# A fused SSM, attention and FFN layer: first steps in a stated order, narrow products for the SSM's outputs, and weights and parameters laid out on the host

## The chip, the cores and the metric

The kernel runs on one core of a Trainium2 chip. The metric is the device time of one execution in microseconds, as the median of several runs. The core has five engines that run their own instruction lists in order: PE (TensorE, products and transposes), DVE (VectorE), ACT (ScalarE), POOL (GpSimd) and SP (SyncE, here only an issuer of DMAs). They wait for one another by semaphores. DMAs are issued by SP, ACT and POOL.

## The reference, cut to what matters

All is float32. There are 256 prompt tokens and 8 samples of 4 tokens, 288 columns together; the model is 2048 wide, the FFN 5632, and the SSM has 64 groups of 16 channels with 64 complex states each.

```python
x = x + 0.5 * swiglu(rms_norm(x, ffn1_norm), ffn1_w_gate, ffn1_w_up, ffn1_w_down)
z = rms_norm(x, mix_norm) @ w_in                       # u, q, k, v, qi, ki, wi, ga, gb
lam_bar = exp(lam * dt); b_bar = ((lam_bar - 1) / lam)[..., None] * b
h = associative_scan(h[t] = lam_bar * h[t-1] + b_bar @ u[t])
y = real(c @ h) + d * u                                # the SSM's outputs
za = gelu(y); a = za * sigmoid(za @ glu_w + glu_b)
b = sparse_attention(q, k, v, top_k by indexer(qi, wi, ki))
x = x + (sigmoid(ga) * (a @ w_branch_a) + sigmoid(gb) * (b @ w_branch_b)) @ w_out
x = x + 0.5 * swiglu(rms_norm(x, ffn2_norm), ffn2_w_gate, ffn2_w_up, ffn2_w_down)
```

## The kernel before

Activations stay in SBUF with channels on the 128 partitions and the 288 tokens as columns. A weight matrix is streamed in chunks of 512 rows by 256 columns (512 KB): SP loads a chunk into a `raw` tile (`fetch`, L208, four buffers), ACT casts it to `whi` (L216) and DVE takes the remainder as `wlo` (L217; `parts`, three buffers each). The activations are split the same way into `hh` and `hl` (or `hi` and `lo`). `project` then makes three products per 128 rows of weights, high by high, high by low and low by high (L240, L241, L242), each 288 columns wide. Of these main products there are 17328 in all, 96 of them from `project_first` (L274 to L276).

PE's instructions run in the order in which the program was written. Those of the other engines are ordered by a scheduler with priorities; `high_priority(offset=FIRST)` lifts the casts and copies that main products need.

`project_first` computes the first 256 columns of the first gate matrix while x arrives. `load_x` loads x in 256-column pieces (`xa`, L304) and the sample rows in pieces of 32 by 128 (`xb`, L309). `turn(k)` transposes the k-th of 16 tiles of x on PE (L316, twice) and brings in the sample columns by products with the identity (L317). ACT scales the tile by the norm's gain into `hh` (L320), DVE forms `hl` (L321), and x itself is copied by ACT for even k and by DVE for odd k (L322). The weights come in steps of 2, 2, 4, 4 and 4 row blocks. The next projection, of w_up, follows directly; for the norm ACT squares the 16 tiles of x (`sq`, L383) and DVE adds them up (`ssq`, L384).

Everything else is side work: Python generators, of which `tick` advances each by one step after every second row block of a projection, so that their instructions fall between main products. `prepare` is such a generator. It loads constants and parameters on ACT's queue, turns norm vectors from rows to columns by transposes on PE (`rows` and `turned`, L347), computes the SSM's discretization, transposes five parameter tables (L653), shuffles b and loads c with short runs (L717, L722), and for each of eight channel blocks `c8` transposes a piece of C (L751) and builds the tables `in`, `chunk`, `out` and `turn`, which go to DRAM. The page table is loaded as `pti` by eight small DMAs (L595) and cast by DVE (L641).

`ssm` is the generator that uses the tables, a software pipeline (`pipe`) of 16 steps n, one each 20 ticks, two steps to a block c8. A stage is given by its lag in ticks. `out` (lag 37) multiplies by `chunk` and `out`: 8 float32 products with the 72 columns of inputs or states as weights and 64 moving columns (L930, L931), after which ACT copies the result, tokens on partitions, to Y. `back` (lag 42) turns a pair's Y with four transposes (L944), and ACT applies GELU. A float32 product is two entries on PE, which the trace's rows count.

Of the kernel before, what the change touches and what calls it, by code (L numbers as in the profile page):

```python
# [13 lines left out]
I32 = mybir.dt.int32  # L14
# [39 lines left out]
L_BIT = 3  # L54

# [63 lines left out]
class Net:  # L119
    def __init__(self, ctx, tc, D):  # L120
# [5 lines left out]
        self.wide, self.turn, self.under_way = True, False, False  # L126
        self.const = ctx.enter_context(tc.tile_pool(name="const", bufs=1))
# [93 lines left out]
    def project(self, w, c0, n, xs):  # L221
# [25 lines left out]
    def project_first(self, w, c0, xs):  # L247

        nc = self.nc
# [3 lines left out]
        raws = {}  # L253

        def fetch(i):
            k0, kt = steps[i]
            raws[i] = self.fetch(w[k0 * P:(k0 + kt) * P, c0:c0 + 256], kt, 256, nc.sync if i else nc.scalar)
        for c, i in enumerate((0, 1, 2, None, 3, None, None, None)):
            if i is not None:
                fetch(i)  # L260
            if c < 7:
                self.load(c + 1)
        xs[1]
        self.warm(2)
        for i, (k0, kt) in enumerate(steps):
            more = steps[i + 1][1] if i + 1 < len(steps) else 0
            if i == 0:
                fetch(4)
            hi, lo = self.parts(raws.pop(i))
            for j in range(2):  # L270
                for k in range(kt):
# [20 lines left out]
    def load_x(self, xp, xs, g):  # L292

        nc = self.nc
        w = 256
        ctx = ExitStack()
        pool = ctx.enter_context(self.tc.tile_pool(name="xin", bufs=1, side="right"))
        rows, some = {}, {}
        self.x = [None] * 16

        def load(c):
            rows[c] = [pool.tile([P, w], F32, name=self.name("xa")) for _ in range(2)]
            for i, a in enumerate(rows[c]):
                nc.sync.dma_start(a, xp[i * P:(i + 1) * P, c * w:(c + 1) * w])  # L304
            if c % 2 == 0:

                some[c // 2] = pool.tile([P, P], F32, name=self.name("xb"))
                for j in range(4):
# [1177 lines left out]
```

## Time and profile before

| | |
|---|---|
| median of 3 runs | 2496.82 us (2496.34 to 2498.28) |
| profiled run | 2496.11 us, its span 2494.3 us |
| PE busy | 2471.9 us, 99% of the span |
| DVE, ACT, POOL busy | 1529.0 (61%), 1083.6 (43%), 171.5 (7%) us |
| mean DMA rate | 177 GB/s |
| weight loads from issue to landing, median | 3.2 to 4.8 us |
| mean granted TensorE clock | 0.999 of full speed |

A PE row of the timeline gives a product's start and duration. Consecutive products overlap, so the time that a product adds is the distance from its start to the next start. Names such as `xa` or `wlo` are the program's tiles. "x4" after a row counts instructions of one kind in a row. What stands in brackets is idle time of the engine ahead of the row, and the last release that ended it.

### The profile page before, as it was taken

The page shows a single profiled execution, that of the slowest core. Times are in us where ns is not written, and L with a number is a line of the kernel's source. Part 1 is how long each engine was busy: PE and PEld are TensorE (multiplying, and loading weights), DVE is VectorE, ACT ScalarE, POOL GpSimd, SP SyncE. Part 2 cuts the span into 40 slices and gives each one's busy share as a digit, 9 for nine tenths or more (in the row PEclk, how much of TensorE's full clock was granted, in tenths as well). Part 3 has the DMA queues.
Part 4 walks back from the last instruction along what each step waited for, and adds up shares of the span by engine and source line. Part 5 has one row for each costly group of instructions (what it writes and reads, how often), then busy time and mean ns, then how long its engine had stood idle before and what let it go on. Part 6 is the DMA issues. An engine that isn't in the chain of part 4 may idle for free.

```text
span 2494.3 us, 46557 instructions
## 1 busy us (share of the span) xinstructions
PE 2471.9 (99%) x18859; PEld 2432.3 (98%) x18859; DVE 1529.0 (61%) x2889; ACT 1083.6 (43%) x1605; POOL 171.5 (7%) x270
## 2 busy tenths in 40 slices
PE   8999999999999999999999999999999999999999
PEld 8999999999999999999899999999999999999999
DVE  6658787875555656789555457556555454554555
ACT  5433334333333445455865634344333333333333
POOL 1001033221000001000023210000000000000000
PEclk9999999999999999999999999999999999999999
DMA  6456666666545655446477676555555555555554
GB/s 198 155 167 156 191 189 193 191 198 193 162 153 178 198 171 184 135 147 201 139 222 234 199 237 224 173 163 167 163 167 168 162 169 166 164 169 163 161 172 134
DMA packets 441962, 441.36 MB, mean 177 GB/s; under 512 B 35002, under 2 KB 432532, under 8 KB 441748
## 3 DMA queue, kind: packets, MB, share of 16 engines
q1 hardware_dynamic: 424608, 413.47, 52.7%
q0 software_dynamic: 11552, 21.32, 2.9%
q10 hardware_dynamic: 5588, 3.61, 0.5%
q8 instruction: 148, 2.42, 0.4%
q14 instruction: 66, 0.54, 0.1%
HBM read 418.48 MB, written 19.83 MB: 176 GB/s over the span
## 4 chain that ended last, share of the span: by engine, by line
PE 93%; DVE 2%; DMA 2%; ACT 1%; issue 1%; POOL 0%; SPq 0%; ACTq 0%; POOLq 0%; DVEq 0%
PE acc L240 16%; PE acc L242 16%; PE acc L241 16%; PE psy L240 13%; PE psy L242 13%; PE psy L241 13%; DVE wlo L217 1%; DMA kv<-in_cache_v,idx 1%; PE aux L1301 1%; DMA raw<-in_ffn_w_gate 0%; DMA cn<-in_ssm_c_re 0%; PE aux L1142 0%; ACT whi L216 0%; PE aux L1347 0%; PE aux L1311 0%
## 5 line engine op out<-in xcount | busy, mean ns | idle before, releaser
L217 DVE TENSOR_TENSOR wlo<-raw,whi 128x1024 fp32r<-128x1024 f32 (+1 forms) x741 | 885.9, 1196 | 752.8 <-ACT whi L216 736.5
L216 ACT CAST whi<-raw 128x1024 fp32r<-128x1024 f32 (+1 forms) x741 | 761.2, 1028 | 1165.3 <-PE acc L241 461.7
L240 PE MATMUL acc<-hh,whi 128*128 128x288 f32 x2240 | 679.1, 303 | 0.0
L242 PE MATMUL acc<-hh,wlo 128*128 128x288 f32 x2240 | 661.1, 295 | 4.6 <-DVE wlo L217 4.6
L241 PE MATMUL acc<-hl,whi 128*128 128x288 f32 x2240 | 661.4, 295 | 0.0
L240 PE MATMUL psy<-hh,whi 128*128 128x288 f32 (+1 forms) x1520 | 454.1, 299 | 0.3 <-DVE g L429 0.3
L241 PE MATMUL psy<-hl,whi 128*128 128x288 f32 (+1 forms) x1520 | 448.5, 295 | 0.0
L242 PE MATMUL psy<-hh,wlo 128*128 128x288 f32 (+1 forms) x1520 | 448.2, 295 | 0.0
L240 PEld LDWEIGHTS acc<-hh,whi 128*128 128x128 f32 x2240 | 421.7, 188 | 8.1 <-issue 7.4
L242 PEld LDWEIGHTS acc<-hh,wlo 128*128 128x128 f32 x2240 | 422.3, 189 | 5.3 <-DVE wlo L217 5.3
L241 PEld LDWEIGHTS acc<-hl,whi 128*128 128x128 f32 x2240 | 422.5, 189 | 1.2 <-issue 0.7
L240 PE MATMUL psy<-hi,whi 128*128 128x288 f32 x992 | 294.0, 296 | 0.0
L240 PE MATMUL acc<-hi,whi 128*128 128x288 f32 x992 | 293.8, 296 | 0.0
L241 PE MATMUL psy<-lo,whi 128*128 128x288 f32 x992 | 292.4, 295 | 0.0
L241 PE MATMUL acc<-lo,whi 128*128 128x288 f32 x992 | 292.4, 295 | 0.0
L242 PE MATMUL acc<-hi,wlo 128*128 128x288 f32 x992 | 292.1, 294 | 0.0
L242 PE MATMUL psy<-hi,wlo 128*128 128x288 f32 x992 | 292.1, 294 | 0.0
L240 PEld LDWEIGHTS psy<-hh,whi 128*128 128x128 f32 (+1 forms) x1520 | 285.3, 188 | 4.2 <-issue 3.3
L241 PEld LDWEIGHTS psy<-hl,whi 128*128 128x128 f32 (+1 forms) x1520 | 285.8, 188 | 1.3 <-issue 1.2
L242 PEld LDWEIGHTS psy<-hh,wlo 128*128 128x128 f32 (+1 forms) x1520 | 285.8, 188 | 0.0
L240 PEld LDWEIGHTS acc<-hi,whi 128*128 128x128 f32 x992 | 186.3, 188 | 1.3 <-issue 1.2
L240 PEld LDWEIGHTS psy<-hi,whi 128*128 128x128 f32 x992 | 186.3, 188 | 1.0 <-issue 0.8
(423 smaller groups left out, 2449.3 us busy)
## 6 DMA issues: line engine op xcount, KB each, us to landing
raw<-in_ffn_w_up SPq DMA_DIRECT2D x176, 512.0 KB, 3.6
raw<-in_ffn_w_gate SPq DMA_DIRECT2D x175, 512.0 KB, 3.5
raw<-in_ffn_w_down SPq DMA_DIRECT2D x160, 512.0 KB, 3.4
raw<-in_w_in SPq DMA_DIRECT2D x120, 512.0 KB, 4.0
raw<-in_w_out SPq DMA_DIRECT2D x32, 512.0 KB, 3.3
raw<-in_ffn_w_down SPq DMA_DIRECT2D x32, 256.0 KB, 2.7
raw<-in_w_branch_a SPq DMA_DIRECT2D x16, 512.0 KB, 3.8
raw<-in_w_branch_b SPq DMA_DIRECT2D x16, 512.0 KB, 3.2
```

What stands on the lines that cost most here:

```text
L216: self.nc.scalar.copy(hi, raw)
L217: self.nc.vector.tensor_tensor(lo, raw, hi.bitcast(F32), op=AL.subtract)
L240: nc.tensor.matmul(out, wh, xh, start=k0 + k == 0, stop=False)
L241: nc.tensor.matmul(out, wh, xl, start=False, stop=False)
L242: nc.tensor.matmul(out, wl, xh, start=False, stop=k0 + k == K - 1)
L1301: nc.tensor.transpose(pk[:, (2 * g + j) * P:(2 * g + j + 1) * P], kr[b4][:, c:c + P], self.ident)
```

## The change

It has four parts.

1. **First steps in a stated order.** Inside `project_first` the orders of SP, ACT and DVE are fixed as written, as PE's is. x is loaded in pieces of 256, 256, 512, 512 and 512 columns, the sample rows in two loads, with 96 zero rows below them that DVE clears, so that they can be transposed like the rest. The copy of tile x lags by one tile (`keep`). The gain arrives as a column. The first two chunks of w_up are loaded and split within `project_first` (`early`). SP issues 15 DMAs up to the last x piece, where there were 33. The constants and parameters of `prepare` go on POOL's queue, each behind a small POOL copy from the last x tile into the target (`held`), which keeps the DMA back until x is complete.
2. **The SSM's outputs.** `out` handles a pair of steps: 4 places t by 3 terms by 4 column groups q, 48 float32 products (96 entries on PE) with 32 columns of weights and 72 moving columns, whose result stands with channels on partitions. Y, its copies and `back` are gone; GELU follows directly. ACT makes one more copy of the inputs (`UU`). The tables `chunk` and `out` are padded to 32 columns, and loaded at lag 24.
3. **Weights in blocks.** The host lays each weight matrix out so that a chunk is 128 runs of 4 KB, where it was 512 runs of 1 KB.
4. **Norms and SSM parameters by partition.** They are laid out on the host with the channel or state on the partition. The transposes of L347 (one of the six is in the first steps), L653 (five) and L751 (eight) are gone with their copies; c is one 512 KB load.

```diff
+def blocks(w, cuts):
+    K = w.shape[0] // P
+    return np.concatenate([w[:, a:b].reshape(K, P, b - a).transpose(1, 0, 2).reshape(-1) for a, b in zip(cuts, cuts[1:])])
...
-            (engine or self.nc.sync).dma_start(raw, src.rearrange("(c p) n -> p c n", p=P))
+            (engine or self.nc.sync).dma_start(raw, src)
...
-            raw = self.fetch(w[k0 * P:(k0 + kt) * P, c0:c0 + n], kt, n)
+            raw = None if self.early else self.fetch(w.part(k0, kt, c0, n), kt, n)
             xs[min(k0 + AHEAD, K) - 1]
-            hi, lo = self.parts(raw)
+            hi, lo = self.parts(raw) if raw is not None else self.early.pop(0)
...
+        with self.tc.manual_schedule(engines={E.SP, E.Activation, E.DVE}):
+            return self.first_steps(w, c0, xs, follows)
...
-        for c, i in enumerate((0, 1, 2, None, 3, None, None, None)):
-            if i is not None:
-                fetch(i)
-            if c < 7:
-                self.load(c + 1)
+        self.load(0)
+        self.load_s(0, 512)
+        for i in range(4):
+            fetch(i)
+            self.load(i + 1)
+            if i == 1:
+                self.load_s(512, D_MODEL - 512)
+        self.warm(9)
+        part(0)
...
                     if more:
                         xs[k0 + kt - 1 + min(more, -(-more * (j * kt + k + 1) // (2 * kt - 2)))]
+                        if j == 0 and k == kt - 1:
+                            part(i + 1)
+                    elif k == 3:
+                        self.early.append(self.parts(self.fetch(follows.part(4 * j, 4, c0, 256), 4, 256, nc.sync)))
...
-            for i, a in enumerate(rows[c]):
-                nc.tensor.transpose(p[:, i * P:(i + 1) * P], a[:, j * P:(j + 1) * P], self.ident)
-            nc.tensor.matmul(p[:, SEQ:NT], some[k // 4], self.ident[:, 32 * (k % 4):32 * (k % 4) + 32], start=True, stop=True)
+            for i, a in enumerate((*rows[k], some[k])):
+                nc.tensor.transpose(p[:, i * P:(i + 1) * P], a, self.ident)
...
-                (nc.vector.tensor_copy if k % 2 else nc.scalar.copy)(x, p[:, :NT])
             self.x[k] = x
+            self.kept.append((nc.vector.tensor_copy if k % 2 else nc.scalar.copy, x, p))
+            if k:
+                self.keep()
...
-        nc.scalar.dma_start(a, src)
+        (nc.scalar if pool else nc.gpsimd).dma_start(a if pool else self.held(a), src)
         return a
+    def held(self, a):
+        b = a if len(a.shape) == 2 else a[:, 0]
+        b = b[:, :min(17, b.shape[1])]
+        self.nc.gpsimd.tensor_copy(b, self.x[15][:b.shape[0], :b.shape[1]])
+        return a
...
-            pti = pool.tile([P, DB], I32, name="pti")
+            pti = self.held(pool.tile([P, DB], I32, name="pti"))
             for n in range(NPG):
-                nc.scalar.dma_start(pti[16 * n:16 * n + 16], D["page_table"][:, n:n + 1].rearrange("b n -> n b").to_broadcast([16, DB]))
+                nc.gpsimd.dma_start(pti[16 * n:16 * n + 16], D["page_table"][:, n:n + 1].rearrange("b n -> n b").to_broadcast([16, DB]))
...
             for o, a in ((rT, r), (cT, c), (sT, s), (frT, fr), (fiT, fi)):
-                p = self.px()
-                nc.tensor.transpose(p[:, :GR], a, self.ident[:GR, :GR])
-                nc.vector.tensor_copy(o, p[:, :GR])
+                nc.gpsimd.tensor_copy(o, a)
                 yield
...
-                p = self.px()
-                nc.tensor.transpose(p[:, :P], cc, self.ident)
...
-                nc.vector.tensor_copy(x.rearrange("p g h -> p (g h)"), p[:, :P])
+                nc.vector.tensor_scalar(x.rearrange("p g h -> p (g h)"), cn[:, c8], sign, None, op0=AL.mult)
...
+            nc.scalar.copy(UU[n % 3], p[:, :2 * M].rearrange("p (q c) -> p q c", q=2))
...
         def out(n):
             c8, h = divmod(n, 2)
+            if h == 0:
+                return
             p = self.py()
-            for j in range(4):
-                m = slice(j * CT * 16, (j + 1) * CT * 16)
-                nc.tensor.matmul(p[:M, m], U[n % 3][:, j // 2, j % 2], C[n][:, j // 2], start=j == 0, stop=False)
-                nc.tensor.matmul(p[:M, m], H[n % 3][:, j, :M], O[n][:, j], start=False, stop=j == 3)
+            for t in range(CT):
+                for x in range(3):
+                    for q in range(4):
+                        k = n - 1 + q // 2
+                        m = slice(t * 32, t * 32 + 32)
+                        if x == 0:
+                            w, v = C[k][:, q % 2, m], UU[k % 3][:, q % 2]
+                        else:
+                            j = 2 * (q % 2) + x - 1
+                            w, v = O[k][:, j, m], H[k % 3][:, j, :M]
+                        nc.tensor.matmul(p[32 * q:32 * q + 32, t * M:(t + 1) * M], w, v, start=t + x == 0, stop=t == CT - 1 and x == 2)
```

The orders below list instructions with the tiles that they write and read. On ACT, at the first tiles of x, before:

```order
L320 ACTIVATE hh_178<-aux_173,col_103 128x288
L539 DMA c_wmask<-in_c_wmask 32x4
L539 DMA c_pick<-in_c_pick 128x34
L322 COPY x_177<-aux_173 128x288
L320 ACTIVATE hh_188<-aux_183,col_103 128x288
L216 CAST whi_234<-raw_128 128x512
```

and after:

```order
L270 CAST whi_147<-raw_109 128x512
L396 ACTIVATE hh_156<-aux_151,col_89 128x288
L396 ACTIVATE hh_165<-aux_160,col_89 128x288
L412 COPY x_155<-aux_151 128x288
L396 ACTIVATE hh_183<-aux_178,col_89 128x288
L396 ACTIVATE hh_196<-aux_191,col_89 128x288
L412 COPY x_182<-aux_178 128x288
```

A copy of x stood ahead of the next tile's `hh`; now it stands behind it, and the constants' DMAs have left ACT. On DVE, around the cast of the page table, early in the second projection, before:

```order
L384 TENSOR_TENSOR ssq_789<-ssq_789,sq_824 128x288
L217 TENSOR_TENSOR wlo_524<-raw_521,whi_523 128x1024
L384 TENSOR_TENSOR ssq_789<-ssq_789,sq_827 128x288
L641 CAST ptf<-pti 128x8
L217 TENSOR_TENSOR wlo_554<-raw_551,whi_553 128x1024
```

and after:

```order
L636 CAST one<-ident 128x12
L271 TENSOR_TENSOR wlo_754<-raw_751,whi_753 128x1024
L271 TENSOR_TENSOR wlo_867<-raw_864,whi_866 128x1024
L714 CAST ptf<-pti 128x8
L715 TENSOR_SCALAR ptf<-ptf,part 128x8
L716 CAST idx_670<-ptf 128x8
```

Before, `wlo_524` is the third chunk of w_up and the cast follows it; after, `wlo_867` is the ninth chunk behind those of `project_first`. On PE at an output of the SSM, before (the last two rows come four times):

```order
L240 MATMUL acc_12383<-hh_10519,whi_12462 128x288
L241 MATMUL acc_12383<-hl_10520,whi_12462 128x288
L242 MATMUL acc_12383<-hh_10519,wlo_12463 128x288
L930 MATMUL psy_12478<-chunk_12145,U_11943 72x64
L931 MATMUL psy_12478<-out_12147,H_11946 72x64
```

and after (for one place t of four; the last two rows come twice for each):

```order
L295 MATMUL acc_12608<-hl_10562,whi_12742 128x288
L296 MATMUL acc_12608<-hh_10561,wlo_12743 128x288
L1021 MATMUL psy_12764<-UU_11942,chunk_12301 32x72 x2
L1021 MATMUL psy_12764<-UU_11943,chunk_12560 32x72 x2
L1021 MATMUL psy_12764<-H_11945,out_12303 32x72 x2
L1021 MATMUL psy_12764<-H_11946,out_12562 32x72 x2
```

The output shape of a product went from 72 by 64 to 32 by 72, with inputs and states as the moving side instead of as weights.

## Rows read from the trace of the kernel before

**Rows 1.** The page: busy us of the engines, and a group of instructions.

```profile
PE 2471.9 (99%) x18859; PEld 2432.3 (98%) x18859; DVE 1529.0 (61%) x2889; ACT 1083.6 (43%) x1605; POOL 171.5 (7%) x270
...
L217 DVE TENSOR_TENSOR wlo<-raw,whi 128x1024 fp32r<-128x1024 f32 (+1 forms) x741 | 885.9, 1196 | 752.8 <-ACT whi L216 736.5
```

**Rows 2.** PE's timeline: start us, duration us, line, operands, count, [idle before, releaser].

```profile
7.26 0.38 PE L274 MATMUL psy<-hh,whi 128*128 128x288 f32 x1
...
15.01 0.33 PE L316 MATMUL aux<-ident,xa 128*128 128x128 f32 x1 [1.81 <-DMA xa<-in_x_prompt]
...
26.00 0.44 PE L316 MATMUL aux<-ident,xa 128*128 128x128 f32 x2 [0.56 <-ACT x L322]
...
26.42 0.38 PE L274 MATMUL psy<-hh,whi 128*128 128x288 f32 x1
...
32.80 0.29 PE L240 MATMUL acc<-hh,whi 128*128 128x288 f32 x1
32.93 0.29 PE L241 MATMUL acc<-hl,whi 128*128 128x288 f32 x1
...
40.55 0.40 PE L242 MATMUL acc<-hh,wlo 128*128 128x288 f32 x1 [1.09 <-DVE wlo L217]
...
46.16 0.40 PE L242 MATMUL acc<-hh,wlo 128*128 128x288 f32 x1 [2.16 <-DVE wlo L217]
...
255.51 0.40 PE L242 MATMUL acc<-hh,wlo 128*128 128x288 f32 x1 [1.33 <-DVE wlo L217]
```

**Rows 3.** Busy us by window: PE, PEld, DVE, ACT, POOL, granted clock, DMA share, GB/s.

```profile
48.00:51.30 3.30, 3.30 (x16) 3.30 (x16) 3.30 (x14) 1.08 (x2) 0.00 (x0) 0.54 0.85 253
```

**Rows 4.** ACT's groups in 0 to 32.8: busy us, mean ns, idle before, releaser.

```profile
L320 ACT ACTIVATE hh<-aux,col 128x288 fp32r<-128x288 f32 x16 | 7.7, 505 | 1.3 <-PE aux L317 1.3
L216 ACT CAST whi<-raw 128x1024 fp32r<-128x1024 f32 (+1 forms) x7 | 6.5, 925 | 5.0 <-DMA raw<-in_ffn_w_gate 4.9
L322 ACT COPY x<-aux 128x288 f32<-128x288 f32 x8 | 3.2, 399 | 5.1 <-DVE hl L321 5.1
```

**Rows 5.** SP's timeline, the issue of the last x loads.

```profile
18.95 0.90 SPq L304 DMA_DIRECT2D xa<-in_x_prompt  x2
```

**Rows 6.** ACT's timeline, four of the squares.

```profile
31.83 1.43 ACT L383 ACTIVATE sq<-x 128x288 f32<-128x288 f32 x4
```

**Rows 7.** DVE's timeline, the cast of the page table.

```profile
44.78 0.17 DVE L641 CAST ptf<-pti 128x8 f32<-128x8 int32 x1 [3.91 <-DMA pz<-in_ssm_lambda_re]
```

**Rows 8.** POOL's timeline, the issue of four loads of b.

```profile
233.54 3.06 POOL L717 DMA_DIRECT2D b<-in_ssm_b_re  x4 [200.47 <-DVE dd L727]
```

**Rows 9.** PE's timeline around an output of the SSM.

```profile
1047.96 0.28 PE L930 MATMUL psy<-chunk,U 128*72 128x64 f32 x2
...
1048.96 0.38 PE L240 MATMUL acc<-hh,whi 128*128 128x288 f32 x1
1049.18 0.29 PE L241 MATMUL acc<-hl,whi 128*128 128x288 f32 x1
```

**Rows 10.** PE's timeline at the four transposes back.

```profile
1118.30 0.42 PE L944 MATMUL psy<-ident,Y 72*128 72x72 f32 x4
1118.52 0.38 PE L240 MATMUL acc<-hh,whi 128*128 128x288 f32 x1
```

**Rows 11.** PE's timeline at products with 32 columns of weights.

```profile
313.49 0.43 PE L805 MATMUL aux<-G,b 128*32 128x64 f32 x16
313.85 0.40 PE L240 MATMUL psy<-hi,whi 128*128 128x288 f32 x1
...
1280.27 1.07 PE L1311 MATMUL aux<-kt,qz 128*32 128x256 f32 x16
1281.28 0.40 PE L240 MATMUL acc<-hh,whi 128*128 128x288 f32 x1
```

**Rows 12.** PE's timeline at a transpose of a parameter table (L653, at 184.26).

```profile
184.03 0.30 PE L242 MATMUL psy<-hh,wlo 128*128 128x288 f32 x1
...
184.46 0.40 PE L240 MATMUL psy<-hh,whi 128*128 128x288 f32 x1
```

More of the change, by code (lines that the diff above doesn't have):

```diff
@@ L54, with __init__, below, part @@
 L_BIT = 3
+class Blocks:
+    def __init__(self, a, K, first=0):
+        self.a, self.K, self.first = a, K, first
+    def below(self, first):
+        return Blocks(self.a, self.K, first)
+    def part(self, k0, kt, c0, n):
+        K = self.K
+        b = self.a[c0 * K * P:(c0 + n) * K * P].rearrange("(p k n) -> p k n", p=P, k=K)
+        return b[:, self.first + k0:self.first + k0 + kt]
+def blocks(w, cuts):
+    K = w.shape[0] // P
+    return np.concatenate([w[:, a:b].reshape(K, P, b - a).transpose(1, 0, 2).reshape(-1) for a, b in zip(cuts, cuts[1:])])
+def laid(arrays):
+    out = dict(arrays)
+    for name in WEIGHTS:
+        w = arrays[name][0]
+        n = w.shape[1]
+        cuts = [*range(0, C_KI + 1, 256), *range(C_GA, n + 1, 256)] if name == "w_in" else [*range(0, n + 1, 256)]
+        out[name] = blocks(w, cuts)
+    for name in ("ffn1_norm", "mix_norm", "ffn2_norm", "glu_b"):
+        out[name] = np.ascontiguousarray(arrays[name][0].reshape(-1, P).T)
+    for name in ("q_norm", "k_norm"):
+        out[name] = np.ascontiguousarray(arrays[name].T)
+    def parts(re, im):
+        a = np.stack([re.reshape(4, 16, -1), im.reshape(4, 16, -1)], 1)
+        return np.ascontiguousarray(a.reshape(P, *re.shape[1:]))
+    for name in ("ssm_lambda_re", "ssm_lambda_im"):
+        out[name] = parts(arrays[name][0].T, arrays[name][0].T)
+    dt = np.broadcast_to(arrays["ssm_log_dt"][0], (64, GR))
+    out["ssm_log_dt"] = parts(dt, dt)
+    c = [arrays[f"ssm_c_{s}"][0].transpose(2, 0, 1).reshape(64, 8, P) for s in ("re", "im")]
+    del out["ssm_c_im"], out["ssm_c_re"]
+    out["ssm_c"] = parts(*c)
+    return out
+WEIGHTS = {"ffn1_w_gate": 16, "ffn1_w_up": 16, "ffn1_w_down": 44, "ffn2_w_gate": 16, "ffn2_w_up": 16, "ffn2_w_down": 44,
+           "w_in": 16, "glu_w": 8, "w_branch_a": 8, "w_branch_b": 8, "w_out": 16}
 def constants():
@@ L323, in turn, with keep @@
             self.x[k] = x
+            self.kept.append((nc.vector.tensor_copy if k % 2 else nc.scalar.copy, x, p))
+            if k:
+                self.keep()
             if k == 15:
+                self.keep()
                 ctx.close()
             return hi, lo
-        load(0)
-        self.load = load
+        self.load, self.load_s = load, load_s
         return Late(16, turn)
+    def keep(self):
+        copy, x, p = self.kept.pop(0)
+        with self.tc.high_priority(offset=FIRST):
+            copy(x, p[:, :NT])
@@ L610, in prepare @@
             yield from self.wait(30)
-            for key, row in cols:
-                setattr(self, key, self.turned(mc, row, row.shape[0]))
-                yield
-            dt = self.exp(pool, ldt, [GR, 1])
+            yield from self.wait(5)
+            dt = self.exp(pool, ldt, S)
             are, aim = T(), T()
             for a, l in ((are, lre), (aim, lim)):
-                nc.vector.tensor_scalar(a, l, dt, None, op0=AL.mult)
+                mul(a, l, dt)
             r = self.exp(pool, are, S)
@@ L851, in ssm @@
         M = DB + NC
-        V, I, C, O, E, Y = ({} for _ in range(6))
+        V, I, C, O, E = ({} for _ in range(5))
         U = [pool.tile([P, 2, 2, M], F32, name=self.name("U")) for _ in range(3)]
+        UU = [pool.tile([P, 2, M], F32, name=self.name("UU")) for _ in range(3)]
         H = [pool.tile([P, 4, M + 1], F32, name=self.name("H")) for _ in range(3)]
@@ L952, in ssm @@
-        yield from self.pipe(16, every, (0, load), (4, by_chunk), (9, by_place), (13, into), (13, load2), (13 + S_OUT, out), (18 + S_OUT, back))
+            v = p[:, :NT].rearrange("p (t c) -> p c t", t=CT)
+            y = u[c8]
+            for o, i in ((slice(0, SEQ), slice(DB, M)), (slice(SEQ, NT), slice(0, DB))):
+                nc.scalar.activation(y[:, o].rearrange("p (c t) -> p c t", t=CT), v[:, i], AF.Gelu_apprx_tanh)
+            za.append(y)
+        yield from self.pipe(16, every, (0, load), (4, by_chunk), (9, by_place), (13, into), (24, load2), (13 + S_OUT, out))
```

174 lines of the change are left out of this document (82 added, 92 removed).

## The prediction

> **What bounds the kernel now.** I read the busy table first. PE is busy through 99% of the span [rows 1], so the time is PE's program laid end to end: 17328 main products of 288 columns that stand 0.13 us apart (the starts 32.80 and 32.93 in [rows 2]), which makes 2253 us by that rounding, then the small products between them, and the few waits. An edit can win in three ways only: take small products off PE, make them shorter, or end a wait. So I went through PE's timeline, looking at starts and not at durations, since the durations overlap. The first 33 us hold most of the waits. From the first product at 7.26 to the first of the second projection at 32.80 pass 25.54 us, with a wait of 1.81 us for x (row 15.01) and smaller ones on ACT and DVE (row 26.00). [...]
>
> **Part 1, the first steps.** The reader should see that the 25.54 us have three portions. 96 products at 0.13 are 12.5. Fourteen of the sixteen x tiles are transposed after 7.26; one takes 0.42 us from its first transpose to the product behind it (26.00 to 26.42), together 5.9. The remaining 7.1 are waits. ACT and DVE hand x over in lockstep: ACT's copy of x waits 5.1 us in all for DVE's half of the same x tile [rows 4], and the next tile's ACT work is queued behind that copy. SP issues its last two x loads only at 18.95 [rows 5].
> The change lets the x copy lag one tile behind, so ACT has the next scaled half (0.51 us) to do meanwhile; the 5.1 us leave the chain. SP issues x and the first weights in 15 entries instead of 33, at 0.45 each (0.90 for two in [rows 5]), so the last x load is out at about 7.5 us. The wait at 15.01 then goes. The sample rows of x become one transpose instead of two narrow products: three transposes of one kind, which I put at 0.33 (four of 72 columns take 0.22 in [rows 10], so 0.055 each, near 0.10 at 128 columns): 4.6 in all. What is late next: ACT. In the second step it owes four scaled halves, two copies and a short cast, 4 x 0.51 + 2 x 0.40 + 0.6 = 3.4 us, and DVE's half behind them, while PE has 12 x 0.13 + 4 x 0.33 = 2.9. With the split of that step's weights that leaves waits of 2.0 to 3.5 us. I take 3.5, since the handover of each tile still passes through both engines. First product at 7.1, so the second projection begins at 7.1 + 12.5 + 4.6 + 3.5 = 27.7. **Term A: -5.1 us** (-2 if half the waits come back, -8 if nearly none).
> DVE also clears 4096 columns of sample rows at its start. That is done before its first split, which waits for a weight load anyway; if it were late, the first product would be.
>
> **Part 2, behind the first steps.** Before, the two waits and the slow clock cost 1.09 + 2.16 and, at 0.54, 16 products in 3.30 us where 2.1 would do [rows 2, 3]: with the edges 1.3. Together 4.55. They have two sources. ACT squares x (0.36 each, four in 1.43, [rows 6]) ahead of the weight cast, and DVE stops in order at the page-table cast, which waits 3.91 us for parameters that were loaded late [rows 7], with the split queued behind it and PE behind the split.
> After the change the first two chunks of the second projection are split early and the page-table cast stands behind nine of its weight splits instead of three. POOL now issues those parameter loads, after x is complete at about 24 us. Its issues cost 0.77 each (3.06 for four, [rows 8]), so twenty of them with the copies ahead are out by about 42 and the table has landed before 50; the cast is due near 55. But the third chunk's cast still stands behind sixteen squares: on ACT from about 25.0, one copy 0.4, two casts 2.0 ([rows 4]), sixteen squares 5.8, two result copies 0.7, the cast 1.0, DVE's half 1.2 ([rows 1]) = 36.1. PE has 48 products, 6.2, and two more before it needs that low half: 27.7 + 6.2 + 0.26 = 34.2. So a wait of about 1.7 to 1.9 stays; I take 1.7. **Term B: -2.9** (0 if the clock falls again and the wait is 3, -4.5 if it vanishes).
>
> **Part 3, transposes that the new layouts make needless.** One parameter transpose costs PE 184.03 to 184.46 less the 0.13 that the products take anyway, 0.30, and 0.1 on the product behind (as 1049.18 after 1048.96 in [rows 9]): 0.40 [rows 12]. There are five of these and five narrower ones for the norms (a sixth lies ahead of the first product), somewhat cheaper: 3.8. The eight of C follow a product directly, as in [rows 10], where one takes about 0.055, and 0.09 on the next product: 1.1 (3.2 at most, by [rows 12]). **Term C: -4.9** (-4 to -7).
>
> **Part 4, the SSM's outputs.** Before, one step is 16 entries of 64 columns, 1047.96 to 1048.96, 1.00, with 0.09 on the next product [rows 9]; two steps and the four transposes back (0.22 in [rows 10], and 0.09 again) make 2.49 us, eight times 19.9. After, 96 entries of 72 columns with 32 columns of weights, that go round the four column groups. The trace has this pattern twice [rows 11]: 16 entries of 64 columns take 0.36 to the next main product, 16 of 256 columns 1.01. The difference is 0.65 for 4 rounds of 192 more columns, 0.85 ns per column and round, so that 64 columns are 54 ns a round, 0.22 for four, and 0.14 is a fixed part. 24 rounds of 72 columns are 1.47; with the 0.14 and edges of 0.1 ahead and behind (as in [rows 9]): 1.8. The other end has nothing fixed: 0.36 / 4 is 90 ns a round, 102 for 72 columns, 2.4 + 0.2 = 2.6. I take 1.85, close to the first, because the two rows differ by columns alone. **Term D: 8 x (1.85 - 2.49) = -5.1** (+1 to -5.6).
> The copies of Y leave ACT, one copy per step joins; neither is waited for. The chunk and output tiles are twice as wide and are loaded 13 ticks ahead, which covers some 20 us.
>
> **Part 5, the rest.** Weights in blocks: PE waits for a weight load nowhere after the first 30 us, its late splits were late on ACT and DVE. Longer runs may land sooner but nobody waits: 0. SSM parameters: DVE has some more small operations, and eight shuffles and seven products of b now stand ahead of one split where fewer did; the wait at 255.51 (1.33, [rows 2]) may go or double. **Term E: +0.5** (-1 to +2).
>
> **Sum.** -5.1 - 2.9 - 4.9 - 5.1 + 0.5 = -17.5. The profiled run took 2496.11 us (its span 2494.3 and 1.8 around it): 2478.6. The median lies 0.7 above the profiled run: 2479.3.
>
> **Rivals.**
> 1. The narrow products run one after the other. Then each entry costs what one costs in [rows 9], 1.00 / 16 = 62 ns, 96 of them 6.0 and 0.33 around: 6.3 instead of 1.85, eight times +35.6, giving 2515, slower than before. It decides from 38 ns an entry (17.5 / 8 = 2.19 more than 1.85). For it: these products share all 128 rows, and they accumulate in one bank. Against it: [rows 11] have the same rows and column groups at 0.36 / 16 = 22 ns even with the fixed part. Chance 0.05. [...]
> 2. The first steps gain nothing: the handover of x between ACT and DVE, or the loads (which now come at once on the same engines), set the pace as before, and the waits of part 2 stay too. A and B fall out: 2487.3. For it: ACT's and DVE's work in this stretch is the same, and 15.01 was a wait for a load. Against: the 5.1 us of waiting for the other engine [rows 4] are plainly order. Chance 0.13.
> 3. The block layout makes the main products closer, by relieving memory. Half a nanosecond on 17328 is 8.7: 2470.6. Against: the spacing in [rows 2] is the same 0.13 while loads run hard. Chance 0.08.
> 4. POOL's queue is late: the page table or the b parameters come after DVE's due place, DVE stops in order with splits behind it and PE behind those, as in [rows 7]. Two such waits of 2 to 3 us: +5, 2484.3. Chance 0.08.
>
> **How the numbers follow.** The forecast has 0.66. Its own range, with A to E off by part of their bounds at once, is 2474 to 2485. To hold 8 in 10, it is stretched to rival 2 above and rival 3 below: 2469 to 2488; rival 1 and the far tails stay out. This kernel's measurement tells 0.2% from nothing, about 5 us, so faster is under 2491.8: the forecast, rivals 3 and 4 and nearly all of rival 2, 0.90; the same 0.05 (rivals 2 and 4 together); slower 0.05 (rival 1).
>
> **What would show it.** A: the first product of the second projection at 25 to 30 us, and no wait on x of over 1 us. B: one wait near 35 for the low half, none on the page-table cast, and whether the clock falls behind it. C: no transposes at 80 to 185 us and about 294. D: an output burst of some 1.5 to 1.6 us to the next main product, eight of them; 2.5 or more breaks the term, 6 is rival 1. E: the wait near 255. The prediction is wrong if the spacing of the main products itself moves, which I can't read from the diff: 0.1% of it is 2.3 us.

## The result, and the profile after

| | before | after |
|---|---|---|
| median of 6 runs | 2496.58 us (2495.2 to 2499.78) | 2480.14 us (2479.21 to 2480.46) |
| span of the profiled run | 2494.3 us | 2477.4 us |

The ratio is 0.9932 with a 95% interval of 0.9919 to 0.9944: 16.4 us faster, where 17.5 were forecast (2479.3). The total is nearly right, but by luck: it is a sum of errors of both signs, as a table by stage shows. It is worked out from PE's timelines: when the first main product starts, the 97th (the first of w_up), and so on, and how much the stage between two of them became shorter.

| start of main product | 1 | 97 | 201 | 2001 | 6901 | 10501 | 17328 |
|---|---|---|---|---|---|---|---|
| before, us | 7.26 | 32.80 | 51.78 | 298.12 | 960.06 | 1579.54 | 2488.96 |
| after, us | 6.91 | 32.12 | 47.06 | 290.01 | 952.54 | 1563.05 | 2472.28 |
| gain in the stage | -0.4 | -0.3 | -4.0 | -3.4 | +0.6 | -9.0 | -0.2 |
| forecast for it | | A -5.1 with the one before | B -2.9 | C, E -4.4 with the next | | D -5.1 | 0 |

So the first steps gave 0.7 us instead of 5.1, the stretch behind them a little more than forecast, the transposes less, and the stage of the SSM and the attention almost twice its term.

PE's timeline of the changed kernel, start, duration, line, operands and [idle before, releaser]. It answers to [rows 2]:

```profile
6.91 0.40 PE L341 MATMUL psy<-hh,whi 128*128 128x288 f32 x1
...
10.46 0.40 PE L341 MATMUL psy<-hh,whi 128*128 128x288 f32 x1 [0.61 <-ACT whi L270]
...
13.51 0.41 PE L393 MATMUL aux<-ident,xa 128*128 128x128 f32 x2 [0.88 <-DVE x L412]
...
16.55 0.40 PE L341 MATMUL psy<-hh,whi 128*128 128x288 f32 x1 [1.39 <-ACT whi L270]
...
17.81 0.40 PE L343 MATMUL psy<-hh,wlo 128*128 128x288 f32 x1 [0.73 <-DVE wlo L271]
...
23.45 0.40 PE L343 MATMUL psy<-hh,wlo 128*128 128x288 f32 x1 [0.60 <-DVE wlo L271]
...
29.08 0.40 PE L343 MATMUL psy<-hh,wlo 128*128 128x288 f32 x1 [0.60 <-DVE wlo L271]
...
32.12 0.29 PE L294 MATMUL acc<-hh,whi 128*128 128x288 f32 x1
...
39.73 0.40 PE L296 MATMUL acc<-hh,wlo 128*128 128x288 f32 x1 [0.78 <-DVE wlo L271]
...
218.74 0.40 PE L296 MATMUL acc<-hh,wlo 128*128 128x288 f32 x1 [1.11 <-DVE wlo L271]
```

The waits for x loads are gone, as forecast. In their place PE waits at the beginning of each step for that step's split weights. ACT's groups from 0 to 32.12 us (busy, mean ns, idle before with its releaser), against [rows 4]:

```profile
L396 ACT ACTIVATE hh<-aux,col 128x288 fp32r<-128x288 f32 x16 | 7.7, 501 | 8.4 <-PE aux L393 8.4
L270 ACT CAST whi<-raw 128x1024 fp32r<-128x1024 f32 (+1 forms) x7 | 6.4, 929 | 2.8 <-DMA raw<-in_ffn_w_gate 2.8
L412 ACT COPY x<-aux 128x288 f32<-128x288 f32 x8 | 3.2, 396 | 0.6 <-DVE hl L397 0.6
```

The lag did what it was read to do: the copy's 5.1 us of waiting became 0.6. But the idle time stayed on the engine; it is now 8.4 us in front of the scaled halves, for PE's transposes (1.3 before), while PE stands and waits for ACT's cast of the weights.

An output of the SSM, one of eight. Five stand alone like this one and agree within 0.01 us; in the other three a few other products share the gap:

```profile
1104.18 0.29 PE L296 MATMUL acc<-hh,wlo 128*128 128x288 f32 x1
1104.41 0.33 PE L1021 MATMUL psy<-UU,chunk 128*32 128x72 f32 x8
1104.56 0.44 PE L1021 MATMUL psy<-H,out 128*32 128x72 f32 x16
...
1106.06 0.40 PE L294 MATMUL acc<-hh,whi 128*128 128x288 f32 x1
1106.30 0.29 PE L295 MATMUL acc<-hl,whi 128*128 128x288 f32 x1
```

From 1104.18 to 1106.30, the main product, the burst and the next main product, pass 2.12 us; less twice the 0.133 of a main product that is 1.85 us.

### The profile page after: what moved, and what is told of

It is laid out like the page before. It is cut to its first block, busy times and chain, and to the rows that moved or that the text cites. A ratio compares the mean times of both kernels' runs of the same rounds, so it can differ in the third digit from the quotient of the medians.

```text
span 2477.4 us, 47535 instructions
## 1 busy us (share of the span) xinstructions
PE 2460.5 (99%) x19304; PEld 2421.0 (98%) x19304; DVE 1530.5 (62%) x2915; ACT 1085.4 (44%) x1626; POOL 201.9 (8%) x319
## 4 chain that ended last, share of the span: by engine, by line
PE 94%; DVE 2%; DMA 2%; ACT 1%; issue 1%; POOL 0%; SPq 0%; DVEq 0%; POOLq 0%; ACTq 0%
PE acc L294 17%; PE acc L295 16%; PE acc L296 16%; PE psy L294 13%; PE psy L295 13%; PE psy L296 13%; DVE wlo L271 1%; PE aux L1380 1%; PE psy L1021 0%; DMA pz<-in_ssm_lambda_im 0%; PE aux L1221 0%; PE aux L1426 0%; PE aux L1390 0%; DMA kv<-in_cache_v,idx 0%; DMA b<-in_ssm_b_im 0%
```

## Experiments

All are edits of the changed kernel, except one that is an edit of the kernel before.

### When a step's weights are split

Theory "order": PE waits for the split because it is queued on ACT and DVE behind work that itself waits for PE's transposes. Rivals: the loads are late, or ACT and DVE are simply full. Two kernels write the split of the next step earlier.

```diff
             if i == 0:
                 fetch(4)
+            if more:
+                part(i + 1)
...
-                        if j == 0 and k == kt - 1:
-                            part(i + 1)
```

> The changed kernel, but inside the first steps the split of the next step's weights is written at the start of a step and no longer behind its first half, so that on ACT and DVE it stands ahead of the scaled halves and copies of the x tiles that PE transposes during the step. In the changed kernel PE waits 0.61 and 0.19 (at 10.46 and 11.18), 1.39 and 0.73 (16.55, 17.81), 0.60 (23.45) and 0.60 us (29.08) for whi or wlo at the starts of steps, 4.1 us. Theory 'order': these waits exist because the split is queued on ACT behind work that waits for PE itself. Then most of them go, the second projection begins at 28 to 29.5 us instead of 32.12, and the time is 2476 to 2478. Rival 'loads': the weights land late (DMA share 1.02 from 10 to 15 us); then the second projection still begins near 32 and the time stays at 2480. Rival 'engines full': the waits come back in front of hl or hh, the gain is under 1.5 us, 2479.

Measured: 2478.11 us (2477.86 to 2480.17), the time at the edge of what "order" expected, but the second projection at 31.93: there far short of it. The waits for whi and wlo are gone from PE's timeline, and others stand in their place:

```profile
11.03 0.33 PE L393 MATMUL aux<-ident,xb 128*128 128x128 f32 x1 [0.54 <-DMA xb<-in_x_sample]
15.27 0.66 PE L393 MATMUL aux<-ident,xa 128*128 128x128 f32 x2 [3.18 <-DVE x L412]
26.46 0.41 PE L393 MATMUL aux<-ident,xa 128*128 128x128 f32 x2 [0.54 <-DVE x L412]
```

On ACT's timeline the cause of the long one is a cast that now stands in front of the tiles and waits for its load:

```profile
12.03 1.04 ACT L270 CAST whi<-raw 128x1024 fp32r<-128x1024 f32 x1 [1.99 <-DMA raw<-in_ffn_w_gate]
```

While PE stood in this wait, at 13.35, the granted clock fell to the lower level (0.50 of full speed in the kernel before from 48 to 51 us), for 6.8 us. By window (busy us of PE, PEld, DVE, ACT, POOL, then granted clock, DMA share, GB/s):

```profile
12.00:20.00 8.00, 4.82 (x22) 4.75 (x22) 4.97 (x8) 4.91 (x9) 0.00 (x0) 0.58 0.87 338
```

So for the chunk of the third step "loads" is right too: an order that is too early runs into the load.

```diff
-                        if j == 0 and k == kt - 1:
+                        if j == 0 and k == kt // 2 - 1:
                             part(i + 1)
```

> As split_start, but the next step's split is written in the middle of the first half of a step (behind its first row block in steps of 2, its second in steps of 4). Theory 'order': a part of the gain, the second projection begins between 28.5 and 31 us, the time is 2477 to 2479.5. Under 'loads' it stays at 32 and 2480. If the long DVE split (1.2 us) in front of the tiles' low halves hurts, this one is faster than split_start.

Measured: **2474.69 us** (2474.37 to 2476.68), ratio to before 0.9914 (0.9898 to 0.9931): 5.4 us faster than the changed kernel, faster than expected, and the fastest of all. The second projection begins at 29.24, as "order" has it:

```profile
10.01 0.40 PE L343 MATMUL psy<-hh,wlo 128*128 128x288 f32 x1 [0.32 <-DVE wlo L271]
11.52 0.33 PE L393 MATMUL aux<-ident,xb 128*128 128x128 f32 x1 [0.89 <-DMA xb<-in_x_sample]
13.45 0.41 PE L393 MATMUL aux<-ident,xa 128*128 128x128 f32 x2 [0.87 <-DVE x L412]
15.63 0.40 PE L343 MATMUL psy<-hh,wlo 128*128 128x288 f32 x1 [0.28 <-DVE wlo L271]
...
29.24 0.30 PE L294 MATMUL acc<-hh,whi 128*128 128x288 f32 x1
```

The 1.39, 0.73, 0.60 and 0.60 us of the changed kernel have become 0.28 and nothing of note, and the first load is not yet asked for too early. "Order" holds, with the load as its limit. Of the gain in the trace, 4.6 us, 2.9 stand there: 2.5 between the first product and the 97th, the edit's own part, and 0.4 because the first product came earlier, which the edit doesn't touch. 1.4 more come from the spacing of main products up to the 6901st (133.37 and 133.19 ns on average in the two stages of the changed kernel, 133.14 and 132.99 here; the cause of that is open), the rest from single waits.

### The first steps as a whole, and the early chunks

`project_first` and `load_x` were put back as they were, with the new weight layout:

> The changed kernel with the first steps as they were: loads of x in 256 columns, sample rows in pieces of 32 by 128, two products for them, copies of x not lagging, order of SP, ACT and DVE left to the scheduler, no early chunks; the gain as a column, the block layout, the parameter loads on POOL and all other parts as changed. By the two traces the first steps gave 0.7 us up to the second projection; if nothing else hangs on them, this kernel loses 0.7 there and what the early chunks give: 2481 to 2484.5. If the part as a whole is worth the 8.0 us of the predicted terms A and B, it is at 2488.

Measured: 2480.0 us (2477.98 to 2480.97), the same as the changed kernel. Its second projection begins at 34.37, 2.3 later, but the two stages behind it are 1.1 and 1.0 shorter. As written, this part of the change is worth nothing that can be measured.

The early chunks of w_up alone were taken out:

```diff
-                    elif k == 3:
-                        self.early.append(self.parts(self.fetch(follows.part(4 * j, 4, c0, 256), 4, 256, nc.sync)))
```

> The changed kernel without the two early chunks: the first two w_up chunks are loaded and split by the ordinary projection again, everything else as changed (the parameter loads on POOL, the page-table cast late). Theory 'early': the early split is what ended the waits of 1.09 and 2.16 us behind the first steps; then they come back in part, together 1.5 to 3 us, perhaps with the lower clock behind them (1.3 more), and the time is 2481.5 to 2484.5. Rival 'page table': the waits went because the page-table cast and its loads went elsewhere; then the wait near 39.7 us stays at about 0.8 and the time stays within 1 us of 2480.

Measured: 2479.61 us (2477.73 to 2479.97). "Early" falls: without it the stage from 97 to 201 takes 13.90 us, less than the 14.94 with it, and the wait at 39.73, which "page table" expected to stay, does not occur at all. "Page table" is what is left, and the kernel before with that one thing changed tests it:

```diff
-            nc.vector.tensor_copy(ptf, pti)
+            self.tc.keep_in_program_order(nc.vector.tensor_copy(ptf, pti))
```

> The kernel before with one thing changed: the cast of the page table (L641) keeps its place in the program's order, so that on DVE it no longer stands between the splits of the third and fourth chunk of w_up, 44.78 us. Theory 'page table': that cast was the wait of 2.16 us at 46.16 and, by it, the lower clock from 47.65 to 51.1 us; both go, 3.5 us less up to the 200th main product, 2493. The wait of 1.09 at 40.55 stays. Rival 'the parameters are late anyway': the next parameter product (L570) waits for its loads in the cast's place, and the time stays at 2496.5.

Measured: 2493.79 us (2492.97 to 2495.77) against 2495.29 in the same session, ratio 0.9995 (0.9985 to 1.0004), so in time alone unclear. In the trace the stage from 97 to 201 takes 15.46 us instead of 18.98, 3.5 less; up to the 201st product it is 3.0 less, where 3.5 were expected. The two waits and the clock behind them:

```profile
40.52 0.40 PE L242 MATMUL acc<-hh,wlo 128*128 128x288 f32 x1 [0.49 <-DVE wlo L217]
47.93 0.40 PE L242 MATMUL psy<-hh,wlo 128*128 128x288 f32 x1 [0.76 <-DVE wlo L217]
```

```profile
47.00:52.00 5.00, 4.24 (x32) 4.08 (x31) 4.79 (x16) 2.72 (x5) 0.00 (x0) 1.00 0.79 258
```

The 2.16 us went down to 0.76 and the clock stays at the full level, 1.00 against 0.66 in the same window before (0.54 in the narrower one of [rows 3]). The 1.09, which was to stay, went down to 0.49, because this run was 0.6 later by the 97th: its own fall of the clock came at 15.5, while PE waited for x (0.999 on average over its profiled run, and 1.00 in every window from 30 to 60 us). And 0.7 came back, with a wait of 1.6 us at 75.59, so that 2.3 stay at the end.

The cast's place is not the whole cause, for what the rival named happened too. DVE still stops for the late parameters, at the parameter product in the cast's stead:

```profile
46.08 0.28 DVE L570 TENSOR_TENSOR pz<-pz 64x128 f32<-64x128 f32 x1 [3.75 <-DMA pz<-in_ssm_lambda_re]
```

The edit let one more split go ahead of that stop, at 40.75, and that spared most of the wait. In the changed kernel the stop is still there, and longer:

```profile
59.82 0.17 DVE L714 CAST ptf<-pti 128x8 f32<-128x8 int32 x1 [5.06 <-DMA pz<-in_ssm_lambda_re]
```

PE has no idle span of over 0.05 us between the one at 39.73 and one of 0.36 us at 72.59, so nothing waits behind it: DVE was ahead by then, its splits at 47.12, 50.33 and 53.53 had themselves waited 1.8 to 2.0 us each for ACT's half.

Both findings put together:

> The changed kernel with both findings: the next step's weight split in the middle of a step's first half, and no early chunks of w_up. If both add up: 5.4 us less by the first and 0.6 by the second, 2474; up to the 200th main product 43.0 to 43.5 us, where split_mid alone stands at 43.94. If the splits of w_up now fall among the last x tiles, it is as split_mid, 2474.7, or up to 1 us slower.

Measured: 2478.64 us (2477.63 to 2479.36), 4 us slower than split_mid, against both expectations. DVE's timeline shows a part of it:

```profile
24.69 2.36 DVE L271 TENSOR_TENSOR wlo<-raw,whi 128x1024 fp32r<-128x1024 f32 x2 [0.66 <-ACT whi L270]
26.97 0.51 DVE L395 SCALAR_TENSOR_TENSOR hl<-aux,col,hh 128x288 fp32r<-128x288 f32 x1
27.40 0.45 DVE L410 COPY x<-aux 128x288 f32<-128x288 f32 x1
27.76 1.21 DVE L271 TENSOR_TENSOR wlo<-raw,whi 128x1024 fp32r<-128x1024 f32 x1
28.89 0.51 DVE L395 SCALAR_TENSOR_TENSOR hl<-aux,col,hh 128x288 fp32r<-128x288 f32 x1
```

and PE's, what follows:

```profile
29.46 0.44 PE L342 MATMUL psy<-hl,whi 128*128 128x288 f32 x1 [1.26 <-DVE hl L395]
29.70 0.44 PE L343 MATMUL psy<-hh,wlo 128*128 128x288 f32 x1
29.94 0.44 PE L341 MATMUL psy<-hh,whi 128*128 128x288 f32 x1
```

With their place not written down, the scheduler puts w_up's splits in front of the last tiles' low halves; in no_early PE is later and waits only 0.24 for that, here it waits 1.26. Behind the wait, from 29.67 on, the granted clock is at the lower level for 3.4 us (0.66 on average from 29 to 34), and the products stand 0.24 apart, where they stood 0.13 apart ahead of it. The stated order holds the splits back. What that is worth is less than the 4 us: of 4.8 us between the two traces, 1.9 stand between the first product and the 201st, 0.9 ahead of the first product, and 2.1 in the two stages up to the 6901st, where the main products have the changed kernel's spacing again (133.41 and 133.19 ns).

The second load of sample rows cut in two, on top of this:

> mid_no_early with the second load of the sample rows cut in two (512 and 1024 columns), the larger one an x piece later. In split_mid PE waits 0.89 us for the sample rows at 11.52 us, behind a DMA share of about 1 from 10 to 15 us. If that load is late only because it is large and shares the engines, the second projection begins 0.5 to 1 us earlier than in mid_no_early; if the next weight chunk or x piece is late in its place, nothing changes.

Measured: 2477.96 us (2475.74 to 2479.36). The stage from 1 to 97 takes 24.66 us instead of 25.39, but only because more of the same fall of the clock (0.84 on average from 30 to 40 us) lies behind the 97th: from the first to the 201st product it is 39.3 us against 39.4. The run could not decide either, as mid_no_early has no wait of PE for the sample rows to begin with.

### The narrow products

The loop over the four column groups became the outermost one, so that 24 entries in a row use the same columns.

```diff
-            for t in range(CT):
-                for x in range(3):
-                    for q in range(4):
+            for q in range(4):
+                for t in range(CT):
+                    for x in range(3):
```

> The changed kernel with the loops of the narrow products exchanged: all 24 entries of one column group, then the next group; the same 96 entries with the same operands. Theory 'going round the column groups makes them overlap': now neighbours share the group, each entry costs up to the 62 ns of the old output entries, a burst is up to 6.3 us instead of 1.85 and the time up to 2515; at least twice the 15 ns an entry, +12, 2492. Rival 'any narrow product is cheap' (32 weight columns are loaded quickly, behind the running product): burst at 1.85 and time at 2480 as before.

Measured: 2508.2 us (2508.08 to 2510.58), 28 more. The same 96 entries:

```profile
1107.98 0.29 PE L296 MATMUL acc<-hh,wlo 128*128 128x288 f32 x1
1108.21 0.31 PE L1021 MATMUL psy<-UU,chunk 128*32 128x72 f32 x2
1108.36 0.41 PE L1021 MATMUL psy<-H,out 128*32 128x72 f32 x4
...
1113.68 0.41 PE L294 MATMUL acc<-hh,whi 128*128 128x288 f32 x1
```

From the first narrow entry to the next main product pass 5.47 us, 57 ns an entry, against 1.65 and 17 ns in the changed kernel. The starts of the single entries, which the rows above merge, say how. In q_outer neighbours stand 61 to 65 ns apart, also where the place t changes and with it the columns that are accumulated, so a shared accumulator is not the reason; only where the column group changes are some of them closer, down to 6 ns. In the changed kernel four entries start within 20 to 35 ns, and from one such four to the next it is some 62 ns again. So in either order the entries of one column group stand some 62 ns apart, and four groups ran side by side where neighbours go to different ones; all entries here share all 128 rows. The price of rival 1 exists for neighbours in one group.

The old form of the outputs, with the padded tables:

> The changed kernel with the old form of the SSM's outputs: 16 entries of 64 moving columns per step with inputs or states as weights, Y, its copy by ACT, and four transposes per pair; the padded tables and the other parts stay. Theory 'term D alone': an output pair costs 2.49 us instead of the measured 1.85, eight times: +5.1, 2485.2. Rival 'more than its products': from 953 to 1563 us the changed kernel gains 9.0 us, 3.9 more than D; if the shorter ACT and DVE chain of the new form gave these too, this kernel is at 2488 to 2489.

Measured: 2489.58 us (2488.39 to 2491.75), 9.4 more: "more than its products". The stage from 6901 to 10501 takes 620.6 us against 610.5. PE's idle spans of over 50 ns in it add up to 8.2 us before, 4.1 after, and 7.7 here; those with ACT as the releaser to 5.3, 0.9 and 5.3. The longest ones are back at their places:

```profile
1197.49 0.22 PE L1287 MATMUL aux<-bias,idb 128*128 128x128 bf16 x1 [1.00 <-ACT e L1295]
...
1205.14 0.27 PE L1287 MATMUL aux<-bias,idb 128*128 128x256 bf16 x1 [1.10 <-ACT e L1295]
...
1255.66 0.66 PE L1381 MATMUL aux<-ident,kv 128*128 128x128 f32 x4 [1.85 <-ACT kt L1383]
```

The attention waits for ACT. The 3.6 us more of idle spans, the 5.0 of the products and a fall of the clock at 1257 behind the last of these waits (0.999 on average over the profiled run) are about the 10.1 that the stage lost. ACT changes its activation table 37 times before and in old_out, at 1.28 us each, and 34 times after. ACT's timeline ahead of the first of the waits above:

```profile
1193.00 1.28 ACT L1453 ACT_TABLE_LOAD   x1
1194.29 0.44 ACT L1453 ACTIVATE z<-z 128x288 f32<-128x288 f32 x1
...
1195.34 1.28 ACT L1295 ACT_TABLE_LOAD   x1
1196.63 0.37 ACT L1295 ACTIVATE e<-aux,st 128x128 f32<-128x128 f32 x1
```

A sigmoid (L1453) goes between two exponentials here, and two table loads with it; the exponential behind them is what PE waits for. One explanation is the place of the GELU:

> The changed kernel with the GELU of an output pair five ticks later, at its old lag of 42 ticks, so that it falls on ACT where it fell before; the narrow products stay. old_out lost 9.4 us where its products cost 5.1. Theory 'table loads': the other 4 us are waits of PE for ACT (at 1202.8, 1210.5, 1218.3 and 1261.0 us before) that came from ACT changing its activation table 37 times instead of 34, since GELU then falls between exponentials and sigmoids; with GELU back at the old place there are 37 loads again and the time is 2483.5 to 2484.5. Rival 'Y': the waits came from the copies of Y and the transposes, or from where the longer bursts put everything; then this kernel stays within 1.5 us of 2480.

Measured: 2480.48 us (2480.01 to 2481.65), 34 table loads, 4.1 us of idle spans. The GELU's place is not what turns 34 loads into 37. But as the loads did not come back, this run doesn't say whether they make the waits: every profile with 37 has 7.7 us or more of idle spans in this stage, every one with 34 at most 5.4, and in old_out the loads stand in front of the waits. That is an argument and not a test. What brings loads and waits back with the old form, the copies of Y on ACT, the transposes, or the order that the scheduler then finds for ACT, stays open; that they come with the old form is shown.

### Transposes and layout

> The changed kernel with the eighteen removed transposes put back on PE at about their old places (five narrow ones for the norms, five for the parameter tables, eight for C), their results unread and without the copies that followed. Theory 'term C': +4.9, 2485. Rival 'they hide in waits or behind neighbours': less than +2, under 2482.

Measured: 2486.3 us (2484.37 to 2487.17), 6.2 more (5.2 in the profiled run), but not all of it is the transposes. Up to the 6901st product the trace lost 2.7 us; the distances around the eighteen transposes add up to 3.2 us and not 4.7, since the five for the parameter tables cost only 0.11 each here, where they cost 0.40 before. They are not the same products. A transpose of before, and one of this run:

```profile
184.26 0.27 PE L653 MATMUL aux<-ident,ex 64*128 64x64 f32 x1
```

```profile
180.51 0.27 PE L730 MATMUL aux<-ident,cs 128*64 128x128 f32 x1
```

With the new layout the table stands on 128 rows where it stood on 64. By this the prices sort: on 1, 8, 16 or 64 rows 0.34 to 0.40 us (before and here), on all 128 rows 0.11 to 0.12 (the eight for C, before and here, and these five). So the run puts thirteen of the eighteen back about as they were, 2.7 us of term C's 4.7; the other five are priced by the trace of before alone. The rest of the loss came later: one burst of narrow products took 1.8 us longer than in the changed kernel, without a releaser.

```profile
1287.34 0.28 PE L1028 MATMUL psy<-UU,chunk 128*32 128x72 f32 x3 [0.24 <-issue]
...
1288.23 0.34 PE L1028 MATMUL psy<-UU,chunk 128*32 128x72 f32 x4 [0.30 <-issue]
1288.99 0.27 PE L1028 MATMUL psy<-UU,chunk 128*32 128x72 f32 x2 [0.42 <-issue]
```

> The changed kernel with the weight matrices as they are given, so that a chunk is 512 runs of 1 KB again. Theory 'the layout is worth nothing': within 1 us of 2480. Rival 'it makes main products closer': +8, 2488. Other rival: in the changed kernel's trace the main products of the first 950 us stand 0.2 to 0.6 ns farther apart than before; if the layout does that, this kernel is 1.5 to 3 us faster, 2477 to 2478.5.

Measured: 2482.98 us (2482.73 to 2485.11), 2.8 more, between the expectations. The main products' mean spacing is the same to 0.03 ns in both stages (133.40 and 133.19 ns), so neither rival holds, and "worth nothing" allowed 1 us. In the profile the loss is 1.3 us up to 97, with a fall of the clock in it,

```profile
16.00:22.00 6.00, 4.63 (x23) 4.38 (x24) 2.62 (x4) 1.88 (x4) 0.00 (x0) 0.72 0.66 207
```

and one burst that took 1.9 us longer, as above. Neither needs the old layout: gelu_later has the same fall with weights in blocks (0.79 on average from 16 to 24 us), more_turns the burst. All four runs were slower than any of the changed kernel, so the loss is no scatter; what the layout has to do with it is open.

## Why the prediction was right, point by point

**Term A** (-5.1) was wrong by 4.4, more than its own bounds. The step that failed is the 3.5 us taken for the remaining waits. 96 products and 14 tiles cost what was said: a tile takes 0.33 (from 8.57 to the next product at 8.81, and 0.09 behind). From 6.91 to 32.12 are 25.2 us; less 12.7 and 4.6 that leaves 7.9 of waits, counted by distances. The working removed the copy's 5.1 us of idle ACT from the chain, but the idle time of an engine in a lockstep is a consequence: the loop PE, ACT, DVE, PE had a second link, the split of the next step behind the tiles, and that became the longest. It stood in the order of the changed kernel and was counted as 0.6 us of work, not as an order. split_mid shows it: that link moved gave 2.5 us back. Its 5.4 us that are left are still above 3.5; there PE waits for the sample rows and for DVE's copy of x as well. Rival 2 was right about this part, though for another reason than it named.

**Term B** (-2.9, measured -4.0) was right in the waits that go and in that one stays (0.78 instead of 1.7). What before_cast_late shows is that the place of DVE's stop for the late parameters made the wait of 2.16 and the slow clock behind it, 3.0 us up to the 201st product. The working had the stop itself end, with the table landed before 50; it did not, DVE stood until 59.82, and the term came out because PE had split chunks in hand. The early chunks, which the working counted on too, had no part in it.

**Term C** (-4.9) was right as a price: by distances, ten transposes cost 3.8 us before and eight 0.9, together 4.7. The two stages gained only 2.8, as the main products there stand 0.36 and 0.29 ns farther apart on average than before (133.01 and 132.90): on 1786 and 4862 of them that is 2.1. The last sentence of the prediction named this risk; the layout does not cause it, and what does is open. Why the prices differ was read wrongly: not by whether a transpose follows a product directly, which all do, but by the rows on which it stands do the prices of these traces sort, 0.34 to 0.40 us on 1 to 64 rows and 0.11 to 0.12 on 128. E was small (a wait of 1.11 at 218.74, at another product, for the 1.33 at 255.51), but its 0 for the weights in blocks is not borne out: without them the kernel took 2.8 us more, from a cause that is open.

**Term D** (-5.1) was right to the hundredth, 1.85 us a pair. Two rows that differed in their columns alone gave the price of a third size. With each entry at rival 1's 62 ns the burst would have taken some 6 us; entries with the same rows and other columns overlapped in the changed kernel, 17 ns each, and those with the same columns stood some 62 ns apart, there and in q_outer. The working's 0.85 ns per column and round, 61 ns for 72 columns, is the 62 ns of a column group.
What D missed is nearly as large as D: 3.9 us more in its stage, since the waits of the attention for ACT went from 5.3 to 0.9 us with the old form gone. The prediction said of ACT's copies that nobody waits for them, having looked only at the SSM's own chain.

**Rival 3** did not occur. **Rival 4** did, as far as DVE goes: POOL was late (it issued the page table from 43.67 to 49.43 and the lambda loads from 50.19), and DVE stopped for 5.06 us; but PE did not wait behind it, so its price was nothing. The sum came out by luck, since the shortfalls of A and of C with E, 4.4 and 1.6, stand against 3.9 from the attention and 1.1 from B.

## What to carry to other kernels

When two engines hand work to each other through a third, idle time in front of one step says where the loop closes now, not what its removal gives: list every link of the loop in its new order, the weights' preparation too, and take the longest. Moving one line by half a step took 2.5 us out of the first steps, where their whole rewriting was worth nothing that could be measured; too early an order loses it again, as it waits for its load. A stop of an engine costs what its consumers have not in hand: DVE's stop for late parameters was longest, 5.06 us, where it cost nothing. And an operation removed from a shared engine can give as much to another stage that waits for that engine as to its own.

## What the hardware showed that was not expected

Entries with 32 weight columns, 72 moving columns and all rows stood some 62 ns apart in one column group, and four groups ran side by side: 17 ns an entry in a burst of 96 that goes round the groups, 57 ns in one that goes through them one after another.

A transpose between main products cost 0.11 to 0.12 us when it stood on all 128 rows, and 0.34 to 0.40 when it stood on 1 to 64, although it then had fewer moving columns. (Four in a row on 72 rows, at 1118.30 before, cost 0.30 together.)

Apart from the end of a run, a fall of the granted clock, to 0.50 of full speed in the kernel before from 48 to 51 us, lasted 3.4 us each time in seven profiles and 6.8 us in split_start (on average over the profiled run 0.999 in the seven, 0.998 in split_start, 1.0 in the others), always in the first 50 us or behind a wait of the attention (old_out, at 1257). PE had waited shortly before or was still waiting: 2.16 us in before, 1.26 in mid_no_early, 1.85 in old_out, 3.18 in split_start. A fall did not follow every wait: the changed kernel waits 1.39 us at 16.55 and keeps the full clock in its profile (1.00 from 12 to 20 us), gelu_later, with the same first steps, loses it (0.79 from 16 to 24).

A burst of narrow products took 1.8 and 1.9 us longer in two profiles of ten (more_turns, no_blocks), each time the sixth of the eight, with idle spans of PE for which the profile shows no releaser (0.24, 0.30 and 0.42 us in more_turns).
